# A 32-byte unused tile in front of the h tiles of a two-layer attention/Hyena step: where the operands of the main matmuls begin in memory

## The chip, the cores and the metric

The kernel runs on one core of a Trainium2 chip. The metric is the device time of one execution in microseconds (us). Three timed runs of the kernel before gave 1501.36, 1505.44 and 1506.03 us, a median of 1505.44 us. Traces are of one profiled execution.

## What is computed

One inference step of a two-layer backbone. A trunk of 384 tokens of width 2048 (256 latent tokens, then 128 context tokens) passes through two layers. Each layer does the following, with weights of its own:

```
shift, scale, gate = split(silu(c) @ w_ada + b_ada)          # one set for latent, one for context tokens
h    = rmsnorm(x, norm_g) * (1 + scale) + shift
proj = h @ w_in                                               # 2048 -> 7168: q|k|v|gate_att|hyena x0,x1,v|gate_hy
att  = attention(q, k, v, cached context keys) * silu(gate_att)
hy   = hyena(x0, x1, v) * silu(gate_hy)                       # short conv, then a long conv through an rfft
x    = x + gate * (concat(att, hy) @ w_out)                   # 2048 -> 2048
```

At the end a last RMS norm gives both outputs, and the context keys and values of both layers are outputs as well. Inputs and outputs are float32.

## The kernel before

**Split products.** TensorE multiplies the type `float32r` (fp32r below) in one pass, but with fewer bits than float32. So the kernel splits every large operand in two: a high part, which is the value rounded to fp32r, and a low part, which is the rest. A product `h @ w` is then three matmuls into one PSUM bank: high times high, low times high, high times low. The high parts of h lie in four tiles `hh0` to `hh3`, the low parts in `hl0` to `hl3` (class `Quarters`, lines 87 to 100; each tile holds four of the 16 slices of 128 features for all 384 tokens, 6144 bytes per partition). Weights stream from HBM into seven raw buffers of 128x1024 float32 by DMAs on SyncE's queue (`fetch`, line 162); ScalarE writes the high part into a tile `hi` (line 224, four buffers in the pool `hip`), and VectorE the low part into a tile `lo` (line 230, three buffers in `lop`).

**Two forms of the large product.** `b_mm` (lines 789 to 808) makes the parts of the projection that are wanted with tokens on partitions: h is the stationary operand (128 features by 128 tokens) and 512 columns of a split weight move past it (lines 802, 803, 804). It issues 1152 matmuls in all. `a_mm` (lines 822 to 832) makes the others, and the output projection: a 128x128 block of a split weight is the stationary operand and all 384 tokens of h move past it (lines 830, 831, 832). It issues 3 x 1792 = 5376 matmuls.

```
830                mm(b[:, :T], wh, hh[:, kt, :], start=(kt == 0), stop=False)
831                mm(b[:, :T], wh, hl[:, kt, :], start=False, stop=False)
832                mm(b[:, :T], wl, hh[:, kt, :], start=False, stop=(kt == 15))
```

In the trace's names the moving operand stands first: `acc<-hh,hi` is hh moving over the weights hi. Each matmul has a weight load of its own (engine PEld), which runs while the matmul before it streams.

**Order of the work.** The schedule is written by hand (`tc.manual_schedule()`, from line 983): a loop goes through a list of weight units; in each it splits the next unit, issues its 48 (form a) or 36 (form b) matmuls, loads what has a free buffer, and runs some small background work: attention (lines 639 to 707), the FFT products (lines 743 to 784) and the adaLN products, whose matmuls are plain float32 (line 282). In the first 250 us or so the adaLN weights of layer 0 come in, and as h is not yet made, the h tiles serve as eight more landing buffers for 32 loads of 512 KB (`buffer`, line 92, names `hh0b` to `hl3b`). After that h is written by `make_h` (lines 438 to 453) and, before the output projection, by `split_mix` (lines 455 to 457).

**Where tiles lie.** Pools are laid one after the other in each partition's memory, in the order in which they are opened, and every tile begins at a multiple of 32 bytes. So a tile begins either 0 or 32 bytes past a multiple of 64. Worked out from the tile sizes, the pool `one` begins at byte 16512. Its tiles `XM`, `C`, `P1` to `P4`, `acc2`, `scT` and `ones` begin at multiples of 64; `V` and the seven raw buffers (from 107168) begin 32 past one. All `hi` (from 135840, 4096 apart), all `lo` (from 152224), the tiles `tt` and `xz` and the accumulators `pa` also begin 32 past a multiple of 64, and so do the eight h tiles, from 180000 in steps of 6144 up to 223008. Slices within these tiles step by 512, 1536 or 2048 bytes, all multiples of 64. So both operands of each of the 6528 split matmuls begin 32 bytes past a multiple of 64.

Of the kernel before, what the change touches and what calls it, by code (L numbers as in the profile page):

```python
# [10 lines left out]
F32 = mybir.dt.float32  # L11
# [59 lines left out]
def step_kernel(ctx, tc, xT, vec, cst, delta, zfeat, fw, ada, wb, wc, wo, ck, cv, qk1, yT, nk, nv):  # L71
    nc = tc.nc
    pool = lambda name, bufs, **k: ctx.enter_context(tc.tile_pool(name=name, bufs=bufs, **k))
# [13 lines left out]
    class Quarters:  # L87
# [7 lines left out]
        def __getitem__(self, key):  # L95
# [3 lines left out]
                self.t[j] = hpool.tile([128, 4, T], F32R, name=f"{self.name}{j}", tag=f"{self.name}{j}")  # L99
            return self.t[j][p, kt % 4, c]  # L100

    hpool = pool("hpool", 1)
    hh, hl = Quarters("hh"), Quarters("hl")
    C = one.tile([128, C_W], F32, name="C")
# [806 lines left out]
    def ada_units(l, ch, how="P"):  # L911
        return [Unit(ada[l, ch, kc], "ada", l=l, ch=ch, kc=kc, how=how) for kc in range(4)]
# [35 lines left out]
    gap = ada_units(1, 3) + ada_units(1, 7)  # L948
# [254 lines left out]
```

## Time and profile before

| what | value |
|---|---|
| median of 3 timed runs | 1505.44 us |
| the profiled execution's own time | 1502.53 us |
| its span, first to last instruction | 1500.8 us |
| TensorE busy (matmul) | 1470.0 us, 98% of the span |
| TensorE weight loads busy | 1302.7 us, 87% |
| VectorE busy | 976.8 us, 65% |
| ScalarE busy | 586.1 us, 39% |
| GpSimd busy | 51.2 us, 3% |
| moved by DMA | 286.48 MB, 191 GB/s on average |
| granted TensorE clock, mean | 0.995 |

The span is the profiled execution from its first to its last instruction; its own time has 1.7 us more, which lie outside. The recorded duration of a matmul reaches past the start of the next one, because matmuls are pipelined, and its end is modelled. So durations of neighbouring matmuls overlap, and a TensorE that is busy for 98% of the span is not a TensorE at its peak: the pace, from the start of one matmul to the start of the next, says more.

### The profile page before, as it was taken

Reading aid. Unit: us, or ns where it says so; the run is one execution under the profiler, and the core shown is the slowest. Engines: PE = TensorE matmul, PEld = TensorE weight load, DVE = VectorE, ACT = ScalarE, POOL = GpSimd, SP = SyncE. Lnnn points to the kernel's source line nnn. Section 1 sums busy time; section 2 is a strip of 40 time slices with the busy share of each in tenths; the row PEclk is TensorE's granted clock in tenths of the full one; section 3 lists DMA queues with packets and bytes.
Section 4 is the critical chain, followed back from the end, with each engine's and each line's share of the span. In section 5 each row is a group of like instructions: output and inputs, shape, how many; then the busy total and the mean of one; then the engine's idle time right before and its main releaser. Section 6 shows DMA issues by size and latency. Waiting matters only on the chain.

```text
span 1500.8 us, 20718 instructions
## 1 busy us (share of the span) xinstructions
PE 1470.0 (98%) x8032; PEld 1302.7 (87%) x8032; DVE 976.8 (65%) x1619; ACT 586.1 (39%) x975; POOL 51.2 (3%) x94
## 2 busy tenths in 40 slices
PE   9889999999999999999999999999999999999995
PEld 4346778999998999999997888999999999999995
DVE  6734656767876665687687755676677756754443
ACT  2423554555432322343234554554433232244331
POOL 1110000000000000001110000000000000000001
PEclk9999999999999999999999999999999999999998
DMA  9999366444466533569894334533445343544422
GB/s 354 414 356 340 127 230 227 160 143 152 170 228 215 211 128 138 181 198 319 280 321 151 117 129 138 190 133 134 149 168 180 127 176 131 191 150 151 144 97 85
DMA packets 78731, 286.48 MB, mean 191 GB/s; under 512 B 9670, under 2 KB 10504, under 8 KB 78120
## 3 DMA queue, kind: packets, MB, share of 16 engines
q1 hardware_dynamic: 72824, 267.19, 50.4%
q0 software_dynamic: 5808, 17.97, 3.3%
q8 instruction: 63, 1.03, 0.3%
q14 instruction: 36, 0.29, 0.1%
HBM read 271.49 MB, written 13.63 MB: 190 GB/s over the span
## 4 chain that ended last, share of the span: by engine, by line
PE 91%; DMA 5%; DVE 1%; ACT 1%; issue 1%; SPq 0%; DVEq 0%; ACTq 0%
PE acc L830 21%; PE acc L831 21%; PE acc L832 21%; PE acc L802 6%; PE acc L804 6%; PE acc L803 6%; PE adab L282 2%; PE bgb L664 1%; PE bgb L647 1%; DMA hh1b<-in_ada 1%; DMA hl2b<-in_wb 1%; PE bgb L755 1%; DMA hl1b<-in_ada 1%; DMA XM<-in_xT 1%; PE bgb L657 1%; DMA raw<-in_wb 1%
## 5 line engine op out<-in xcount | busy, mean ns | idle before, releaser
L830 PE MATMUL acc<-hh,hi 128*128 128x384 f32 x1792 | 616.7, 344 | 0.0
L831 PE MATMUL acc<-hl,hi 128*128 128x384 f32 x1792 | 605.7, 338 | 0.0
L832 PE MATMUL acc<-hh,lo 128*128 128x384 f32 x1792 | 605.2, 338 | 0.0
L230 DVE TENSOR_TENSOR lo<-raw,hi 128x1024 fp32r<-128x1024 f32 x282 | 343.1, 1219 | 118.0 <-issue 58.5
L224 ACT CAST hi<-raw 128x1024 fp32r<-128x1024 f32 x282 | 294.5, 1045 | 318.3 <-issue 171.2
L830 PEld LDWEIGHTS acc<-hh,hi 128*128 128x128 f32 x1792 | 336.6, 188 | 12.5 <-issue 8.9
L831 PEld LDWEIGHTS acc<-hl,hi 128*128 128x128 f32 x1792 | 336.6, 188 | 3.7 <-issue 1.4
L832 PEld LDWEIGHTS acc<-hh,lo 128*128 128x128 f32 x1792 | 336.5, 188 | 0.0
L358 DVE SCALAR_TENSOR_TENSOR pa<-raw,scT,pa 128x512 f32<-128x512 f32 x330 | 225.9, 744 | 0.0
L802 PE MATMUL acc<-hi,hh 128*128 128x512 f32 x384 | 155.3, 404 | 4.2 <-ACT hh L449 3.9
L803 PE MATMUL acc<-lo,hh 128*128 128x512 f32 x384 | 151.8, 395 | 0.8 <-DVE lo L230 0.8
L804 PE MATMUL acc<-hi,hl 128*128 128x512 f32 x384 | 151.8, 395 | 0.0
L802 PEld LDWEIGHTS acc<-hi,hh 128*128 128x128 f32 x384 | 72.2, 188 | 37.1 <-issue 13.4
L804 PEld LDWEIGHTS acc<-hi,hl 128*128 128x128 f32 x384 | 72.2, 188 | 17.9 <-DVE hl L452 0.9
L803 PEld LDWEIGHTS acc<-lo,hh 128*128 128x128 f32 x384 | 72.3, 188 | 17.0 <-DVE lo L230 1.5
L405 ACT ACTIVATE tt<-XM 128x384 f32<-128x384 f32 x48 | 24.4, 523 | 136.9 <-DVE XM L878 133.4
L878 DVE SCALAR_TENSOR_TENSOR XM<-acc,mod,xo 128x256 f32<-128x256 f32 x64 | 23.8, 413 | 70.1 <-PE acc L832 70.1
L721 DVE SCALAR_TENSOR_TENSOR z<-acc,V,z 128x255 f32<-128x255 f32 (+1 forms) x64 | 25.2, 414 | 38.5 <-ACT z L717 37.4
L721 DVE SCALAR_TENSOR_TENSOR XM<-acc,V,XM 128x255 f32<-128x255 f32 (+1 forms) x64 | 25.2, 414 | 31.9 <-ACT XM L717 30.8
L282 PE MATMUL adab<-raw,scT 128*32 128x512 f32 x248 | 40.4, 604 | 5.0 <-DMA raw<-in_ada 3.3
L721 DVE SCALAR_TENSOR_TENSOR x1c<-acc,V,x1c 128x255 f32<-128x255 f32 (+1 forms) x64 | 25.2, 414 | 27.5 <-ACT x1c L717 26.4
L449 ACT ACTIVATE hh<-tt,mod 128x256 fp32r<-128x256 f32 x64 | 24.7, 446 | 40.9 <-DVE tt L445 40.9
(188 smaller groups left out, 1105.1 us busy)
## 6 DMA issues: line engine op xcount, KB each, us to landing
raw<-in_wc SPq DMA_DIRECT2D x160, 512.0 KB, 3.8
raw<-in_ada SPq DMA_DIRECT2D x150, 512.0 KB, 5.0
raw<-in_wo SPq DMA_DIRECT2D x64, 512.0 KB, 4.4
raw<-in_wb SPq DMA_DIRECT2D x58, 512.0 KB, 4.7
P<-in_ada SPq DMA_DIRECT2D x16, 512.0 KB, 8.0
Hd<-P POOLq DMA_DIRECT2D x24, 256.0 KB, 8.1
P<-Hd SPq DMA_DIRECT2D x4, 1536.0 KB, 8.1
XM<-in_xT SPq DMA_DIRECT2D x4, 768.0 KB, 11.8
```

The lines of the kernel that those rows point to most:

```text
L224: nc.scalar.copy(u.hi[h], u.raw[h])
L230: nc.vector.tensor_tensor(u.lo[h], u.raw[h], u.hi[h].bitcast(F32), ALU.subtract)
L282: mm(part[32 * t:32 * t + 32, :], scT[:, kc * 4 + t, :], u.raw[t // 2][:, (t % 2) * 512:(t % 2 + 1) * 512], start=(kc == 0), stop=(kc == 3))
L358: nc.vector.scalar_tensor_tensor(out=acc, in0=w, scalar=sc, in1=acc, op0=ALU.mult, op1=ALU.add)
L449: nc.scalar.activation(hh[:, kt, a:b], t[:, a:b], AF.Identity, bias=mod[l][:, kt, v:v + 1])
L721: nc.vector.scalar_tensor_tensor(out=out[:, o:o + n], in0=bank[:, i:i + n], scalar=w(k), in1=out[:, o:o + n], op0=ALU.mult, op1=ALU.add)
L802: mm(accs[g][m], hh[:, kt, ms], wh[:, k, :], start=first, stop=False)
L803: mm(accs[g][m], hh[:, kt, ms], wl[:, k, :], start=False, stop=False)
L804: mm(accs[g][m], hl[:, kt, ms], wh[:, k, :], start=False, stop=last)
L830: mm(b[:, :T], wh, hh[:, kt, :], start=(kt == 0), stop=False)
L831: mm(b[:, :T], wh, hl[:, kt, :], start=False, stop=False)
L832: mm(b[:, :T], wl, hh[:, kt, :], start=False, stop=(kt == 15))
```

## The change

One line opens a pool of one buffer, `gapp`, ahead of the pool of the h tiles, and takes a tile of eight floats from it that nothing reads or writes:

```diff
--- before.py
+++ after.py
@@ -99,6 +99,7 @@
                 self.t[j] = hpool.tile([128, 4, T], F32R, name=f"{self.name}{j}", tag=f"{self.name}{j}")
             return self.t[j][p, kt % 4, c]
 
+    pool("gapp", 1).tile([128, 8], F32, name="gap")
     hpool = pool("hpool", 1)
     hh, hl = Quarters("hh"), Quarters("hl")
     C = one.tile([128, C_W], F32, name="C")
```

The eight h tiles then begin 32 bytes later, at 180032 and so on: at multiples of 64. Every other tile stays where it was, `hi` and `lo` among them, which begin 32 bytes past a multiple of 64. The last h tile ends at byte 229184 of a partition. No instruction is added, removed or moved.

## Prediction

> **What bounds the kernel now.** I read the page first: busy times, the row of the granted clock, the chain that ended last, and the costliest groups.
>
> ```profile
> span 1500.8 us, 20718 instructions
> PE 1470.0 (98%) x8032; PEld 1302.7 (87%) x8032; DVE 976.8 (65%) x1619; ACT 586.1 (39%) x975; POOL 51.2 (3%) x94
> PEclk9999999999999999999999999999999999999998
> ...
> PE 91%; DMA 5%; DVE 1%; ACT 1%; issue 1%; SPq 0%; DVEq 0%; ACTq 0%
> PE acc L830 21%; PE acc L831 21%; PE acc L832 21%; PE acc L802 6%; PE acc L804 6%; PE acc L803 6%; PE adab L282 2%; PE bgb L664 1%; PE bgb L647 1%; DMA hh1b<-in_ada 1%; DMA hl2b<-in_wb 1%; PE bgb L755 1%; DMA hl1b<-in_ada 1%; DMA XM<-in_xT 1%; PE bgb L657 1%; DMA raw<-in_wb 1%
> ...
> L830 PE MATMUL acc<-hh,hi 128*128 128x384 f32 x1792 | 616.7, 344 | 0.0
> L831 PE MATMUL acc<-hl,hi 128*128 128x384 f32 x1792 | 605.7, 338 | 0.0
> L832 PE MATMUL acc<-hh,lo 128*128 128x384 f32 x1792 | 605.2, 338 | 0.0
> ...
> L802 PE MATMUL acc<-hi,hh 128*128 128x512 f32 x384 | 155.3, 404 | 4.2 <-ACT hh L449 3.9
> L803 PE MATMUL acc<-lo,hh 128*128 128x512 f32 x384 | 151.8, 395 | 0.8 <-DVE lo L230 0.8
> L804 PE MATMUL acc<-hi,hl 128*128 128x512 f32 x384 | 151.8, 395 | 0.0
> ```
>
> TensorE carries 91% of the chain, and the six lines of split matmuls hold 81% of the span: about 63% in the 5376 matmuls of form a, 18% in the 1152 of form b. They wait for nearly nothing, and the clock is granted in full. So the time is 6528 matmuls times their pace, and one nanosecond a matmul is 6.5 us. To see the pace I took a long stretch of the output projection of layer 1, where little else runs, and one with much VectorE work:
>
> ```profile
> 1340.00:1480.00 140.00, 140.00 (x798) 140.00 (x797) 65.28 (x95) 55.95 (x80) 7.12 (x13) 1.00 0.34 113
> 1290.00:1320.00 30.00, 30.00 (x172) 30.00 (x171) 25.06 (x34) 8.50 (x10) 0.00 (x0) 1.00 0.61 210
> ```
>
> 140 us over 797 weight loads is 175.7 ns a matmul; 30 us over 171 is 175.4. The pace is the same whether VectorE is busy for 47% or for 84% of the stretch, so the other engines do not set it. Nor do they stand close behind: VectorE has 16% left in the fuller stretch, which covers any gain forecast below.
>
> Is that pace all that TensorE can do? The same engine's plain float32 matmuls give a scale:
>
> ```profile
> L657 PE MATMUL bgb<-C,P x96: 270/273/273, 274.5 to 1052.9; 128*128 128x128 f32 x96
> L664 PE MATMUL bgb<-P,P x96: 377/379/483, 284.9 to 1063.0; 128*128 128x256 f32 x96
> L647 PE MATMUL bgb<-P,P x64: 483/486/488, 264.8 to 1042.3; 128*128 128x384 f32 x64
> L830 PE MATMUL acc<-hh,hi x1792: 336/337/741, 256.3 to 1481.9; 128*128 128x384 f32 x200
> L831 PE MATMUL acc<-hl,hi x1792: 331/337/343, 256.5 to 1482.1; 128*128 128x384 f32 x200
> L802 PE MATMUL acc<-hi,hh x384: 390/395/505, 80.5 to 950.7; 128*128 128x512 f32 x192
> L803 PE MATMUL acc<-lo,hh x384: 387/393/505, 81.8 to 950.9; 128*128 128x512 f32 x192
> ```
>
> The columns are minimum, median and maximum in ns. A duration is the pace plus a constant (338 less 175.7 is 162), so differences of durations are differences of pace. Plain matmuls cost (486 - 273) / 256 = 0.832 ns a column over a base of 273 - 128 x 0.832 = 166.5 ns. Split ones cost (393 - 337) / 128 = 0.4375 ns a column, about half. At exactly half, 0.416, and with the same base, 384 columns would take 326 ns and 512 columns 379.5; the means are 338 and 395. So there is an excess of some 12 ns in form a and 15.5 ns in form b, in all 5376 x 12 + 1152 x 15.5 = 82 us. This is an estimate, as it rests on exactly half. Within the split lines durations also spread, 331 to 343 in L831 with the same shapes, while the plain 128 x 384 matmul spreads over 483 to 488. Something makes fp32r matmuls late by a varying amount that plain ones do not show, and where operands lie could be that.
>
> **The change, part by part.** It adds no instruction, wait, semaphore or DMA, and moves none in any queue. It moves eight tiles by 32 bytes. Both operands of every split matmul begin 32 past a multiple of 64 before; afterwards h begins at a multiple of 64 and `hi` and `lo` stay. Five things touch the moved tiles.
>
> (1) Moving h in form a. A row of 384 columns is 1536 bytes, 24 blocks of 64, and begins in the middle of one now, so it touches 25. If reads go by such blocks, the change saves at most one block, 16 columns x 0.4375 = 7.0 ns, and at least nothing; if what counts is a clash with the weight load, which begins at the same distance from a multiple of 64, the whole excess of 12 ns is the bound. Below nothing I take the slow end of L831, 343 against a mean of 338: 5 ns lost. Between 12 gained and 5 lost the nearest row is the spread of these matmuls themselves. The step that the change can most plausibly remove is the varying part, so I take a mean that falls to the floor of the most frequent line, L830's minimum of 336: 338 - 336 = 2 ns, x 5376 = 10.8 us.
>
> (2) h as the stationary operand in form b, with `hi` or `lo` moving from where they were. Here only a clash between the two could change. By the same reading the mean of 395 falls to L802's minimum of 390: 5 ns x 1152 = 5.8 us. The bounds are 15.5 ns gained (17.9 us) and 5 ns lost (5.8 us).
>
> TensorE: Matmul & The Clock Gate, in the Trainium skill, section "Back-to-back issue gap", gives N / 2.4 + 2.5 ns as the gap of isolated warm matmuls: 162.5 ns at 384 columns, where the trace has 175.7. By that figure the excess would be 13.2 ns in form a, about 71 us there, in line with the 12 ns worked out from the rows.
>
> (3) The plain matmuls of line 282 in the startup, with the h tiles as buffers of moving data:
>
> ```profile
> L282 PE MATMUL adab<-P,scT x64: 592/592/617, 712.2 to 808.1; 128*32 128x512 f32 x64
> L282 PE MATMUL adab<-hh2b,scT x16: 592/592/617, 25.1 to 94.2; 128*32 128x512 f32 x16
> ```
>
> `scT` and P begin at multiples of 64, `hh2b` 32 past one, and both rows have a median of 592. So plain matmuls do not care: nothing.
>
> (4) VectorE and ScalarE write h. VectorE's two comparable steps are these:
>
> ```profile
> L452 DVE SCALAR_TENSOR_TENSOR hl<-tt,mod,hh x64: 343/412/486, 67.3 to 837.8; 128x256 fp32r<-128x256 f32 x32, 128x128 fp32r<-128x128 f32 x32
> L445 DVE SCALAR_TENSOR_TENSOR tt<-XM,asc,acc x56: 342/411/485, 73.7 to 836.5; 128x256 f32<-128x256 f32 x28, 128x128 f32<-128x128 f32 x28
> ```
>
> L445 mixes tiles at both distances, L452 has its large tiles all at one, and they take 411 and 412: nothing. ScalarE's writes have no such pair; I give them nothing too, as TensorE covers them, and at most the 3.9 us that L802 waits for them.
>
> (5) The 32 startup loads that land in the h tiles. Three of them stand on the chain:
>
> ```profile
> 9.65 12.49 DMA hl1b<-in_ada
> ...
> 33.66 16.21 DMA hh1b<-in_ada
> ...
> 79.76 14.28 DMA hl2b<-in_wb
> ...
> hh3b<-in_ada SPq DMA_DIRECT2D x5, 512.0 KB, 8.2
> hl3b<-in_ada SPq DMA_DIRECT2D x5, 512.0 KB, 11.2
> ```
>
> The same size takes 8.2 or 11.2 us at the same distance from a multiple of 64, so the queue ahead decides, not the address. I give it nothing; a tenth of the 43 us on the chain, 4 us either way, is the bound.
>
> The sum: 10.8 + 5.8 = 16.6 us less. Against the profiled execution, 1502.5 us with 1.7 us outside the span, that is 1485.9 us; the median of the timed runs is 2.9 us above it, and against 1505.4 the forecast is 1489 us. Its own range is 1468 us (the block's 7.0 ns in form a, 37.6 us) to 1501 us. What is late next is TensorE again.
>
> **Rivals.** *The address does nothing.* One place in the trace has weights and moving data 32 bytes apart already, where attention's values in P2, at a multiple of 64, are loaded while h still streams:
>
> ```profile
> 284.52 0.34 PE L831 MATMUL acc<-hl,hi 128*128 128x384 f32 x1
> 284.52 0.19 PEld L832 LDWEIGHTS acc<-hh,lo 128*128 128x128 f32 x1
> 284.70 0.34 PE L832 MATMUL acc<-hh,lo 128*128 128x384 f32 x1
> 284.70 0.36 PEld L664 LDWEIGHTS bgb<-P,P 128*128 128x128 f32 x2
> 284.87 0.38 PE L664 MATMUL bgb<-P,P 128*128 128x256 f32 x1
> ```
>
> The L832 matmul over which the P weights load takes 0.17 us to the next start, the L831 before it 0.18: no faster by more than the rounding. That speaks for no change. Against it: this load serves a plain matmul, and h still begins in the middle of a block; no fp32r data moves from a multiple of 64 anywhere in this trace. The time would be 1505. The Trainium skill, SBUF — State Buffer, section "Who interferes with whom", goes further: TensorE's two read ports, for moving data and for weights, are independent, and TensorE waits on no one. By that rule the change is worth nothing; the one handover above agrees, and the excess is not explained by it.
>
> *Most of the excess goes.* If equal beginnings are what costs, 43 to 82 us go: 1423 to 1462. For it is that plain matmuls, at half the rate, show no spread; against it the same handover.
>
> *The streams fall out of step, and it is slower.* Now both begin alike. If a weight load that begins half a block off the moving stream meets it in more blocks, each matmul pays what the slow ones pay now, 343 against 338: 5 ns x 6528 = 33 us, 1538; if half of them do, 16 us, 1522. It decides from 0.7 ns a matmul on (4.5 us over 6528), that is, as soon as L831's mean passes 338.7. The spread shows that such a state exists; nothing shows that the change leads there.
>
> *The change doesn't do what it says.* The pool could end elsewhere or not shift h. By the sizes h moves by exactly 32 bytes and still fits, so this is a small part of the no-change case.
>
> **How the numbers follow.** The forecast has 0.38, the large gain 0.08, no change 0.31, slower 0.23. About 0.3%, 4.5 us, is what a measurement of this kernel can tell from no change. So faster is 0.46, same 0.31, slower 0.23. The range runs from 1462, which leaves out the large gain, to 1522, which leaves out the worse half of the slower case.
>
> **What would show it.** In the profile after: L831's median at 336 or less and its spread narrower; L803 near 390; the stretch of the output projection at 174 ns or less a matmul. L282's and L452's rows should stand. The forecast is wrong if L831's mean stays at 338 (no change), if it falls by 7 ns or more in form a with form b unmoved (then the moving operand's own beginning counts), or if it rises to 340 or more. If the time moves while these rows stand, the startup's DMAs were the cause.

## The result, and the profile after

The changed kernel took 1492.74 us (median of 4 runs, 1492.26 to 1494.59), the kernel before 1504.51 us in the runs beside it. The ratio is 0.9926, with a 95% interval from 0.9912 to 0.9941. The profiled execution took 1492.46 us, and its span fell from 1500.8 to 1490.7 us. All line numbers of the changed kernel are higher by one: 831 to 833 are form a (h moves over weights), 803 to 805 form b (weights move over h).

The page of the changed kernel first: span, busy times, and four of the six groups of split matmuls, with count, busy time in us and mean duration in ns.

```profile
span 1490.7 us, 20718 instructions
PE 1461.4 (98%) x8032; PEld 1293.2 (87%) x8032; DVE 976.7 (66%) x1619; ACT 586.2 (39%) x975; POOL 51.1 (3%) x94
...
L831 PE MATMUL acc<-hh,hi 128*128 128x384 f32 x1792 | 613.9, 343 | 0.0
L833 PE MATMUL acc<-hh,lo 128*128 128x384 f32 x1792 | 602.7, 336 | 0.0
L832 PE MATMUL acc<-hl,hi 128*128 128x384 f32 x1792 | 602.6, 336 | 0.0
...
L803 PE MATMUL acc<-hi,hh 128*128 128x512 f32 x384 | 156.2, 407 | 4.2 <-ACT hh L450 3.9
```

Two lines of form a went from 338 to 336 ns and the third from 344 to 343; line 803, which is 802 before, went from 404 to 407. All other engines kept their busy times. The next rows are the same two stretches as before, 10 us earlier. Each has the window, its length, the busy time in us (with the count) of TensorE, its weight loads, VectorE, ScalarE and GpSimd, then the granted clock, the DMA share and GB/s:

```profile
1330.00:1470.00 140.00, 140.00 (x810) 140.00 (x809) 65.66 (x95) 56.84 (x81) 7.11 (x13) 1.00 0.34 114
1280.00:1310.00 30.00, 30.00 (x175) 30.00 (x174) 25.06 (x34) 9.81 (x12) 0.00 (x0) 1.00 0.59 206
```

In 140 us TensorE loads weights 809 times where it had 797, and in 30 us 174 times where it had 171, again whatever VectorE does beside it. The lines one by one (minimum, median, maximum duration, first and last start):

```profile
L832 PE MATMUL acc<-hl,hi x1792: 335/336/342, 256.5 to 1471.7; 128*128 128x384 f32 x200
...
L804 PE MATMUL acc<-lo,hh x384: 388/394/632, 82.0 to 946.6; 128*128 128x512 f32 x192
...
L283 PE MATMUL adab<-hh2b,scT x16: 592/592/617, 25.3 to 94.4; 128*32 128x512 f32 x16
...
L453 DVE SCALAR_TENSOR_TENSOR hl<-tt,mod,hh x64: 341/412/486, 67.4 to 832.8; 128x256 fp32r<-128x256 f32 x32, 128x128 fp32r<-128x128 f32 x32
```

The median of this line of form a fell by 1 ns, and its first matmul still starts at 256.5 us, so the startup gave nothing. L283 and L453 are where L282 and L452 were. The median of L804, which is L803 before, rose by 1 ns. Adding up all intervals from one matmul's start to the next, by the form of the first of the two, shows where the time went:

| us | before | after |
|---|---|---|
| after matmuls of form a | 958.1 | 946.0 |
| after matmuls of form b | 275.9 | 277.9 |
| after all others | 251.5 | 251.6 |

So 12.1 us came from form a, and form b gave 2.0 us back, some 0.5 us of it by its pace and the rest at breaks. The durations hide a part of this. The exact pace comes from the starts: the last stretch of form a runs without a break, and in the kernel before its line 831 has these rows (then the changed kernel's line 832).

```profile
L831 PE MATMUL acc<-hl,hi x284: 336/337/343, 1331.1 to 1480.5; 128*128 128x384 f32 x142
```

```profile
L832 PE MATMUL acc<-hl,hi x285: 336/336/336, 1323.0 to 1470.7; 128*128 128x384 f32 x143
```

Every third matmul is of this line: 149.4 us over 283 x 3 is 176.0 ns a matmul before, 147.7 over 284 x 3 is 173.4 after. The spread from 336 to 343 has become 336 throughout.

### The profile page after: what moved, and what is told of

Its sections match the earlier page's. It is cut to its first block, busy times and chain, and to the rows that moved or that the text cites. A ratio compares the mean times of both kernels' runs of the same rounds, so it can differ in the third digit from the quotient of the medians.

```text
span 1490.7 us, 20718 instructions
## 1 busy us (share of the span) xinstructions
PE 1461.4 (98%) x8032; PEld 1293.2 (87%) x8032; DVE 976.7 (66%) x1619; ACT 586.2 (39%) x975; POOL 51.1 (3%) x94
## 4 chain that ended last, share of the span: by engine, by line
PE 91%; DMA 5%; DVE 2%; ACT 1%; issue 1%; SPq 0%; DVEq 0%; ACTq 0%
PE acc L831 21%; PE acc L833 21%; PE acc L832 21%; PE acc L803 6%; PE acc L805 6%; PE acc L804 6%; PE adab L283 2%; PE bgb L665 1%; PE bgb L648 1%; DMA hh1b<-in_ada 1%; DMA hl2b<-in_wb 1%; PE bgb L756 1%; DMA hl1b<-in_ada 1%; DMA XM<-in_xT 1%; PE bgb L658 1%; DMA raw<-in_wb 1%
## 5 line engine op out<-in xcount | busy, mean ns | idle before, releaser
L803 PE MATMUL acc<-hi,hh 128*128 128x512 f32 x384 | 156.2, 407 | 4.2 <-ACT hh L450 3.9
L804 PE MATMUL acc<-lo,hh 128*128 128x512 f32 x384 | 152.2, 396 | 0.8 <-DVE lo L231 0.8
L803 PEld LDWEIGHTS acc<-hi,hh 128*128 128x128 f32 x384 | 72.5, 189 | 37.4 <-issue 13.4
L804 PEld LDWEIGHTS acc<-lo,hh 128*128 128x128 f32 x384 | 72.6, 189 | 17.6 <-DVE lo L231 1.5
L283 PE MATMUL adab<-raw,scT 128*32 128x512 f32 x248 | 41.0, 610 | 2.7 <-ACT tt L406 1.5
L722 DVE SCALAR_TENSOR_TENSOR x1c<-acc,V,x1c 128x255 f32<-128x255 f32 (+1 forms) x64 | 25.2, 414 | 26.5 <-ACT x1c L718 25.3
```

What stands on the lines that cost most here:

```text
L283: mm(part[32 * t:32 * t + 32, :], scT[:, kc * 4 + t, :], u.raw[t // 2][:, (t % 2) * 512:(t % 2 + 1) * 512], start=(kc == 0), stop=(kc == 3))
L722: nc.vector.scalar_tensor_tensor(out=out[:, o:o + n], in0=bank[:, i:i + n], scalar=w(k), in1=out[:, o:o + n], op0=ALU.mult, op1=ALU.add)
L803: mm(accs[g][m], hh[:, kt, ms], wh[:, k, :], start=first, stop=False)
L804: mm(accs[g][m], hh[:, kt, ms], wl[:, k, :], start=False, stop=False)
```

## Experiments

Below, *distance* is the number of bytes from a weight tile (`hi` or `lo`) to an h tile, modulo 512. All pairs of a kernel share it, as the tiles and the slices within them step by multiples of 512 or begin alike modulo 512. It is 128 before (180000 - 135840 = 86 x 512 + 128) and 160 with the change. Paces are means over all intervals between two neighbouring matmuls of one form, breaks left out, worked out from the starts in each trace: before 175.9 ns in form a and 232.8 in form b, with the change 173.6 and 233.3.

My theory was that the distance between h and the weights sets the pace. The rival was that the moving operand's own beginning does, at a multiple of 64 bytes or not.

**All at multiples of 64, and only the weights there.** Three unused tiles of 32 bytes, ahead of `hip`, `tp` and `hpool`, put weights and h at multiples of 64; the first two alone put only the weights there.

```diff
-    hip = pool("hip", HIB)
+    pool("gapw", 1).tile([128, 8], F32, name="gapw"); hip = pool("hip", HIB)
-    tp = pool("tp", 3)
+    pool("gapt", 1).tile([128, 8], F32, name="gapt"); tp = pool("tp", 3)
-    hpool = pool("hpool", 1)
+    pool("gapp", 1).tile([128, 8], F32, name="gapp"); hpool = pool("hpool", 1)
```

> The tiles hi and lo begin at multiples of 64 as well as the tiles of h, so that h and the weights begin alike again, 0 apart modulo 64, but all at multiples of 64. If the distance between h and the weights counts: the time and the pace of before, about 1504 us, L831 near a mean of 338 ns and 175.7 ns from start to start in form a. If the moving operand's own beginning at a multiple of 64 counts: at least as fast as the change, 1493 us or less, form a at 173.5 ns, and form b, whose moving hi and lo are now at a multiple of 64 for the first time, faster too, by some 2 ns of 395.

> Only hi and lo begin at multiples of 64, h stays 32 past one: 32 apart modulo 64 as in the change, but with the two sides exchanged. If the distance counts: the change's pace, 173.5 ns in form a, about 1493 us. If the moving operand's own beginning counts: form a at the pace of before, 175.7 ns, and only form b faster; about 1502 us.

Measured: 1494.55 us with all at multiples of 64 (ratio 0.9932, 0.9915 to 0.9948), 1489.57 us with the weights alone there (0.9904, 0.9889 to 0.9919). With the weights alone there form a keeps 173.4 ns though h begins 32 past a multiple of 64, as it did before: the moving operand's own beginning, read modulo 64, is not it. But with all at multiples of 64, 0 apart modulo 64, the kernel is faster than before too, with 175.1 ns in form a and 229.2 in form b: my theory, read modulo 64, fails as well.

**A gap of 64 bytes.** The unused tile has 16 floats in place of 8.

```diff
-    hpool = pool("hpool", 1)
+    pool("gapp", 1).tile([128, 16], F32, name="gapp"); hpool = pool("hpool", 1)
```

> The unused tile has 64 bytes in place of 32, so h moves by 64 and begins 32 past a multiple of 64 as before. If beginnings modulo 64 are all that counts: the time of before, 1504 us, and 175.7 ns in form a. If any other move of h does it (a multiple of 128 or 256, or merely another layout): something else than 1504, about 1493 us if a gap of any size is enough.

Measured: 1494.44 us (0.9933, 0.9917 to 0.9950), 174.7 ns in form a and 229.3 in form b. So 64 bytes, which leave everything as it was modulo 64, bring as much as the change's 32. In the two edits above the gaps ahead of `hip` and `tp` had also moved h, by 96 bytes in all in the first and by 64 in the second, without my heeding it. By distance the runs fall in order: the second edit and the change are both at 160, with the same paces; the first edit and this one are both at 192, with paces within 0.4 ns.

**High and low parts apart.** hh in a pool behind 32 unused bytes, hl in one behind 32 more (distances 160 and 192); and `lo` alone moved by 96 bytes, then all behind it by 32 more (distances 256 to `hi`, 160 to `lo`).

```diff
-    hpool = pool("hpool", 1)
+    pool("gapp", 1).tile([128, 8], F32, name="gapp"); hpool = pool("hpool", 1); pool("gapl", 1).tile([128, 8], F32, name="gapl"); hlpool = pool("hlpool", 1)
...
-                self.t[j] = hpool.tile([128, 4, T], F32R, name=f"{self.name}{j}", tag=f"{self.name}{j}")
+                self.t[j] = (hpool if self.name == "hh" else hlpool).tile([128, 4, T], F32R, name=f"{self.name}{j}", tag=f"{self.name}{j}")
```

```diff
-    lop = pool("lop", LOB)
+    pool("gapo", 1).tile([128, 24], F32, name="gapo"); lop = pool("lop", LOB)
-    tp = pool("tp", 3)
+    pool("gapt", 1).tile([128, 8], F32, name="gapt"); tp = pool("tp", 3)
```

> The high parts of h begin at multiples of 64 (32 apart from the weights), the low parts 32 past one (0 apart). In form a two matmuls in three move hh, one moves hl. If each matmul's pace goes by its own moving operand and the weights loaded under it: lines 830 and 832 near the change's pace (173.5 ns), line 831 near that of before (175.7), about 1497 us. If the pace is a pattern over several matmuls that a single odd one in three disturbs: all three lines share a pace, at 176 ns or more, about 1504 us or above.

> Of the weights only lo moves: hi stays at distance 0 modulo 128 from h, lo is at distance 32. In form a, lo is the stationary operand of line 832 and is loaded while line 831 streams. If the clash is between a stream and the weights loaded under it: line 831 goes at the change's 173.5 ns and the others stay near 176, mean about 175. If it is between a stream and its own weights: line 832 does. If one odd matmul in three only shifts a common pattern: all three lines differ from 175.9 by some tenths, with none at 173.5. The time is 1497 to 1505 us by each.

Measured: 1501.63 us (0.9991, 0.9981 to 1.0001) and 1499.44 us (0.9971, 0.9958 to 0.9985). Both have 175.6 ns over form a. The lines 830, 831 and 832 differ, by the step from each to the next matmul (174.9, 176.0, 175.8 ns in the first; 174.1, 175.7, 176.8 in the second), so neither expectation of the first run came true, and in the second the last of its three came nearest. None keeps the 173.5 that a distance of 160 or 256 gives by itself (the next experiment has 256), though the second run has only these two: the pace is a pattern over several matmuls, and mixed distances lose most of the gain. Whether a stream meets its own weights or those loaded under it stays open.

**Gaps of 96, 128, 160 and 192 bytes.** One number of the diff each: 24, 32, 40 or 48 floats, here the second.

```diff
-    hpool = pool("hpool", 1)
+    pool("gapp", 1).tile([128, 32], F32, name="gapp"); hpool = pool("hpool", 1)
```

> An unused tile of 96 bytes: distance 96 modulo 128, not seen so far. h begins at a multiple of 64, as in the change, and is 32 apart from the weights modulo 64, as in the change. If modulo 64 were enough after all: 173.5 ns in form a, 233.3 in form b, 1493 us. If the distance counts modulo 128: free to differ; a pace away from both 173.5 and 233.3 settles it.

> The runs so far have three distances from the weights to h, modulo 128: 0 (the kernel before), 32 (the change, and the exchange of sides) and 64 (all at multiples of 64, and the gap of 64). Runs of one distance have one pace in each form, whatever the beginnings themselves. An unused tile of 128 bytes gives distance 0 modulo 128 again (128 modulo 256 becomes 0). If the distance modulo 128 counts: the kernel before, 1504 us, 175.9 ns in form a and 232.8 in form b. If it counts modulo 256, or if merely the layout of before was unlucky: another pace, and about 1494 us if any move helps.

> An unused tile of 160 bytes: distance 32 modulo 128, as in the change, and the other one modulo 256. If the distance modulo 128 counts: the change's pace, 173.5 ns in form a and 233.3 in form b, 1490 to 1494 us. If modulo 256: a pace not seen yet.

> An unused tile of 192 bytes, the largest that fits: distance 320 modulo 512, which is 64 modulo 256 and not seen yet. So far form b had 232.8 ns at distance 128, 229.2 at 192 and 227.6 at 256, and 233.2 to 233.3 at 160, 224 and 288. If form b goes by whether the distance is a multiple of 64: below 233 here. For form a there is no forecast beyond 173.3 to 176.7; the time is 1485 to 1500 us.

Measured, with all others of one distance:

| distance | kernel | time, us | ratio, 95% interval | form a, ns | form b, ns |
|---|---|---|---|---|---|
| 128 | before | 1504.5 | - | 175.9 | 232.8 |
| 160 | the change | 1492.7 | 0.9912 to 0.9941 | 173.6 | 233.3 |
| 160 | only the weights at multiples of 64 | 1489.6 | 0.9889 to 0.9919 | 173.4 | 233.3 |
| 192 | all at multiples of 64 | 1494.6 | 0.9915 to 0.9948 | 175.1 | 229.2 |
| 192 | gap of 64 | 1494.4 | 0.9917 to 0.9950 | 174.7 | 229.3 |
| 224 | gap of 96 | 1491.0 | 0.9896 to 0.9925 | 173.5 | 233.3 |
| 256 | gap of 128 | 1485.0 | 0.9850 to 0.9883 | 173.5 | 227.6 |
| 288 | gap of 160 | 1496.8 | 0.9929 to 0.9960 | 174.7 | 233.2 |
| 320 | gap of 192 | 1489.8 | 0.9894 to 0.9924 | 173.3 | 233.3 |

The gap of 128 bytes beats both kernels: modulo 128 nothing has moved, so the distance does not count modulo 128 either. The expectation that form b is quick at every multiple of 64 fell at 320.

**The distance alone?** The 128 bytes put ahead of `hip`, so that weights and h move together; and the distance of 256 made with everything 32 bytes further on (8 floats ahead of `hip`, 8 ahead of `tp`, 24 ahead of `hpool`, written as above).

```diff
-    hip = pool("hip", HIB)
+    pool("gapw", 1).tile([128, 32], F32, name="gapw"); hip = pool("hip", HIB)
```

> The unused 128 bytes stand ahead of hi, so that hi, lo and h all move by 128 and the bytes from a weight tile to an h tile are those of the kernel before: 128 modulo 512. The same 128 bytes between the weights and h gave 1485 us. If only the distance from the weights to h counts: the kernel before, 1504 us, 176 ns in form a, 232.8 in form b. If the place of h itself, or any new layout, counts: about 1485.

> The distance of the gap of 128 bytes (256 modulo 512), but with hi, lo and h all 32 bytes further on, so that all begin at multiples of 64 and not 32 past one. If only the distance counts: 173.5 ns in form a and 227.6 in form b, 1485 us. If beginnings at multiples of 64 count as well: away from it; the run with all at multiples of 64 and distance 192 had 175.1 and 229.2.

Measured: 1503.19 us, a ratio of 1.0003 (0.9993 to 1.0012), and 1484.73 us (0.9874, 0.9859 to 0.9889). The two rows here are the last stretch of form a and a stretch of form b, first with both moved by 128:

```profile
L831 PE MATMUL acc<-hl,hi x284: 336/337/343, 1330.2 to 1479.6; 128*128 128x384 f32 x142
...
L803 PE MATMUL acc<-lo,hh x35: 392/392/398, 829.0 to 852.8; 128*128 128x512 f32 x35
```

then with the gap of 128:

```profile
L831 PE MATMUL acc<-hl,hi x285: 331/334/339, 1315.8 to 1463.5; 128*128 128x384 f32 x143
...
L803 PE MATMUL acc<-lo,hh x35: 387/389/396, 822.4 to 845.5; 128*128 128x512 f32 x35
```

The same 128 bytes give 149.4 / 849 = 176.0 ns in one place and 147.7 / 852 = 173.4 in the other; in form b 23.8 / 102 = 233.3 and 23.1 / 102 = 226.5. Three pairs of kernels with one distance and other addresses (160, 192 and 256) agree in both paces within 0.4 ns, and so does a fourth, the kernel before and this control. This control and the gap of 128 even have h at the same byte, 180128, and the kernel before and the gap of 128 have the weights at the same byte, 135840; the paces differ all the same. So it is the distance between the two operands, not where either lies.

**One distance, two paces.** At 192 and 288 form a's mean lies between 173.3 and 176.7. In the trace of the gap of 160 this is no blur: each stretch keeps one of these two paces (at 192 some keep a third, 174.7). The last run, on top of the gap of 160, enters the slow last stretch anew ahead of each of its last 16 units, by one plain matmul of 128 columns.

```diff
-            split(u, 1)
+            split(u, 1); warm(1) if l and u.kind == "o" else None
```

> The kernel with the gap of 160 bytes, in which the last stretch, 862 matmuls of form a without a break, kept a pace of 176.7 ns while other stretches with the same distances kept 173.3. Added: one plain 128x128 matmul ahead of each of the 16 units of that stretch, so that it is entered anew 16 times; nothing else changes. If how a stretch is entered picks one of several paces that the distance allows: some of the 16 pieces keep 173.3, others 176.7. If the addresses alone fix the pace at each place: all stay at 176.7.

It took 1500.41 us in its one run. From the timelines (start, duration in us), first the gap of 160 alone, then with the added matmuls; the lines left out are the matmuls between:

```profile
1351.55 0.34 PE L832 MATMUL acc<-hh,lo 128*128 128x384 f32 x1
...
1359.50 0.34 PE L832 MATMUL acc<-hh,lo 128*128 128x384 f32 x1
```

```profile
1351.02 0.34 PE L832 MATMUL acc<-hh,lo 128*128 128x384 f32 x1
1351.19 0.38 PE L490 MATMUL bgb<-ones 128*128 128x128 f32 x2
...
1351.77 0.34 PE L832 MATMUL acc<-hh,lo 128*128 128x384 f32 x1
...
1359.57 0.34 PE L832 MATMUL acc<-hh,lo 128*128 128x384 f32 x1
```

Both spans hold 45 matmuls: 7.95 / 45 = 176.7 ns without, 7.80 / 45 = 173.3 with. By the starts in the trace all 16 pieces run at 173.3, while the two units just ahead of them, which the edit does not touch, keep 176.7. The expectation had some of the pieces staying slow; none did. So, as far as one run shows, the distance sets which paces exist, and how a stretch is entered picks among them. The added matmuls cost more than they save: the step from line 832 to the next line 832 across one is 1351.77 - 1351.02 = 0.75 us where it is 0.52 without one at the quick pace, 0.23 x 16 = 3.7 us, against 16 x 48 x 3.4 ns = 2.6 us. The run is longer by more than that 1.1 us: its last stretch already begins 2.6 us later, at 1325.9 against 1323.3 us, ahead of any added matmul. That part has no explanation here.

## Why the prediction was right, and where it was not

*The bound.* TensorE's pace in the split matmuls was read rightly as what sets the time; nothing else became late. Of the 16.6 us forecast 11.8 came between the medians and 10.1 in the profiled span.

*Term 1, form a* (10.8 us forecast): right in size and in kind. 12.1 us came, and what went is the varying part, the repeating slow matmul. Its reason was half right. The conditional picture of 64-byte blocks is refuted: with only the weights at multiples of 64 h still begins in the middle of a block, and form a is as fast. The other condition, a clash with the weights, is borne out in so far as the distance to them counts, but not as "begin alike modulo 64": the gaps of 64 and 128 bytes leave them alike and are faster. That this gap brings all of the 10.8 us was in part luck: by the reasoning modulo 64 a gap of 160 bytes is worth the same, and it brings (175.9 - 174.7) x 5376 = 6.5 us in form a.

*Term 2, form b* (5.8 us forecast): this is the step that failed. "By the same reading the mean of 395 falls to L802's minimum of 390" did not happen; form b lost 2.0 us, and its pace went from 232.8 to 233.3 ns. Its quicker patterns exist, at distances 192 and 256, where it does 229.2 and 227.6 ns, but not at 160.

*Terms 3 to 5* (nothing each): L283 and L453 stand, form a starts at the same time, and the three startup loads on the chain took 11.72, 16.22 and 14.43 us where they had taken 12.49, 16.21 and 14.28:

```profile
10.60 11.72 DMA hl1b<-in_ada
...
33.83 16.22 DMA hh1b<-in_ada
79.94 14.43 DMA hl2b<-in_wb
```

*A reading that was too fine.* "A duration is the pace plus a constant" holds only within a few ns. The gap of 128 and the change share 173.4 ns in the last stretch, with median durations of 334 and 336. Counts over a stretch and starts are what to go by.

*No change.* The handover to a plain matmul's weights spoke for it, and misled: it happens once at a time, and the pace is a pattern over several split matmuls. The rule of the Trainium skill, SBUF — State Buffer, "Who interferes with whom", that TensorE's two read ports are independent and that it waits on no one, was read as a forecast of no change, and so read it does not hold here for fp32r: 20718 instructions that differ in nothing but addresses take 1503 or 1485 us by where 128 unused bytes lie. The measurement decides. That the two ports are where the operands meet is not shown, and no run here tests whether TensorE waits on another engine.

*Most of the excess goes.* No distance tried came near it: the fastest, 256, gained 19 us, with form a still at 173.5 ns.

*Slower.* No distance tried made it slower than before. The bound of 343 ns for every matmul was never reached; the slowest pattern seen is 176.7 ns against 176.0.

What stays open: which part of the chip makes the two operands meet, why form a often has the slow pattern of 176.7 ns at 288 and 192, at 160 only in four of the changed kernel's stretches, and at 224, 256 and 320 in none of the traces, and the full period of the distance. It is not 128, since 128 and 256 differ; more than 192 bytes of gap do not fit into a partition beside the other tiles, so nothing beyond 320 was tried.

## What to carry to other kernels

Where TensorE is the bound and streams fp32r data, take its pace from starts over a long unbroken stretch, and look whether neighbouring matmuls of one shape differ. Then try a few distances between the stationary and the moving tiles with an unused tile: each costs one line, and here the best of six gaps gave 1.3% where the first gave 0.7%. Do not stop at the first that helps or trust a modulus that was inferred from it, and move one side at a time, with a control that moves both.

## What the runs showed of the hardware

TensorE settles into repeating patterns. By the starts in the traces, the last stretch of form a in the kernel before repeats five steps, 175, 182, 176, 173 and 174 ns, though the program repeats three lines; with the change every step is 173 or 174; with the gap of 160 four steps repeat, 175, 180, 174 and 178. The paces come out as simple multiples of one time, 6.67 ns. Form a has 173.3, 176.0 and 176.7 ns, 26, 26.4 and 26.5 times 6.67, so that the kernel before loses two such times in every five steps and the gap of 160 two in every four; form b has 226.5 and 233.3 in the rows above, 34 and 35 times. Two more rows of form b, the run with all at multiples of 64 and the one with `lo` moved alone:

```profile
L803 PE MATMUL acc<-lo,hh x35: 387/392/392, 827.4 to 850.7; 128*128 128x512 f32 x35
```

```profile
L803 PE MATMUL acc<-lo,hh x35: 389/393/397, 828.4 to 852.0; 128*128 128x512 f32 x35
```

23.3 / 102 = 228.4 and 23.6 / 102 = 231.4 are 34.3 and 34.7 times. By the prediction's estimate of 0.416 ns a column, 6.67 ns is 16 columns, 64 bytes of a moving row; 384 columns would be 24 such steps and 512 would be 32, so the best patterns found have two steps more in both forms. That TensorE waits for a slot that comes round every 6.67 ns would fit all of this, but no run here shows it.
